# A down projection turned round: activations as the loaded weights, w_down moving, output by token

## Chip, cores and metric

The kernel runs on one core of a Trainium2 chip. The metric is the device time of one execution in microseconds. All times inside the program are counted from the start of the profiled span.

## What is computed

One transformer block over 2048 tokens of 1024 features, in float32: a modulated norm, a mixer of attention over compressed, selected and windowed keys beside a gated linear recurrence, and a feed-forward network with a causal convolution. Six modulation vectors come from one small product. The part that matters here is the end:

```python
mod = (c_act @ ada_w[l] + ada_b[l])[:, None, :]
sh1, sc1, g1, sh2, sc2, g2 = jnp.split(mod, 6, axis=-1)
...
x = x + g1 * (mixed @ w_out[l])
h = _rmsnorm(x, ffn_norm_g[l]) * (1.0 + sc2) + sh2
x = x + g2 * _conv_ffn(h, ffn_w_gate[l], ffn_w_up[l], ffn_conv_w[l], ffn_conv_b[l], ffn_w_down[l])
return _rmsnorm(x, final_norm_g)
```

`_conv_ffn` convolves `h @ w_gate` (2816 features, width 3), takes its silu, multiplies by `h @ w_up` and projects with `w_down` back to 1024 features.

## The kernel before

The program has three stages: the projections (pool "a"), attention with the output projection (pool "t"), and the feed-forward network (pool "f", from line 910). Tokens go in 4 chunks of 512 (`TC`), features in blocks of 128 (`P`).

Every float32 product is made of three matmuls (`mm3`, line 127): each operand is split into a high part (rounded to the matmul's format) and a low part, and high×high, high×low and low×high are summed in PSUM. `split` (line 120) makes the parts: ScalarE copies the high one, VectorE or GpSimd subtracts for the low one. `pe.matmul(ps, a, b)` loads `a` (128×128) as weights and moves `b` through; the trace and the order name the moving operand first (`pd<-gh,wd_0h`: gh moves, wd_0h is loaded).

A chunk of the feed-forward stage runs so:

- 22 blocks f of the gate and up products (lines 931 to 953). `wload` (918) fetches 512 KB of weights on SP's queue and splits it, the low part on GpSimd. Weights are the loaded operand, the normed input `hT` (8 pairs of 128×512) moves; results are features × tokens, in PSUM banks "g" and "u". The convolution, silu and product (940 to 952) leave pairs `gT` (gh, gl), features × tokens.
- the norm of the next chunk's input (`norm_T`, 161, and `norm_k`, 149): x is loaded by tokens, transposed by TensorE into bank "t", scaled into the next `hT`.
- the down projection (963 to 976): for each of 8 blocks d of output features, two weight loads of 704 KB, 66 matmuls with `gT` moving into one bank "d" (features × tokens). ScalarE copies the bank to `yT`, scaled by the column g2. TensorE transposes yT in four 128×128 pieces into bank "t", and VectorE adds each to `O`, the residual by tokens.
- the final norm (978 to 999): after block 6 and again after block 7, squares on ScalarE, a GpSimd power for 1/rms, the gains, and the store of `O`.

The modulation products run as small steps in the projection stage (`ada_steps`, 187, two per call of `ada_next`): steps b = 16 to 23 (g1) make a row, broadcast over 128 partitions by a matmul with ones, and store it to DRAM (`G1_d`); the others make columns of `mod`, among them b = 40 to 47 (g2).

The order of instructions on each engine is set by a scheduler that simulates the program (`schedule_with_timeline_sim`), not by the source. Each engine, and SP's queue of transfers, then runs its list in order; an instruction that waits holds up what is behind it. Tiles with one tag share `bufs` buffers; a new one waits until the oldest is released.

Of the kernel before, what the change touches and what calls it, by code (L numbers as in the profile page):

```python
# [38 lines left out]
ROW = {"gate_b": (0, 24), "cb2v": (24, 88), "fng": (88, 88 + D), "ada_g1": (88 + D, 88 + 2 * D)}  # L39
NROW = 88 + 2 * D  # L40
# [13 lines left out]
def hymba_block(ctx, tc, x, vecs, rows, ada, w_in, w_v, lru_w, cmp_w1, cmp_w2, w_out, w_gu, w_dn,  # L54
# [43 lines left out]
    G1_d = dr.tile([P, D], F32, name="G1_d")  # L98
    cact = cst.tile([P, KT], F32, name="cact")
# [49 lines left out]
    def norm_k(pl, pp, xs, c, k, Acol, Bcol, hbufs):  # L149
        ps = pp.tile([P, TC], F32, name=f"tp{c}_{k}", tag="t", bufs=2)  # L150
# [36 lines left out]
    def ada_steps(pl, pp, caz, b):  # L187
# [5 lines left out]
        if 16 <= b < 24:  # L193
            ps = pp.tile([P, P], F32, name=f"ap{b}", tag="g", bufs=2)
            pe.matmul(ps, ones, r, start=True, stop=True)
            gsl = slice((b - 16) * P, (b - 15) * P)
            ar = pl.tile([P, P], F32, name=f"ar{b}", tag="adrow", bufs=1)
            o = ROW["ada_g1"][0] + (b - 16) * P
# [711 lines left out]
    with tc.tile_pool(name="f", bufs=1, reuse_waits="tile") as pl, tc.tile_pool(name="fp", bufs=1, space=PSUM, reuse_waits="tile") as pp:  # L910
        reserve(pl, ("hh", 2048, 8), ("hl", 2048, 8), ("x", 4096, 6), ("hf", 2048, 2), ("junk", 2048, 1),
                ("raw", 512 * (NF // 2), 2), ("wh", 512 * (NF // 2), 2), ("wl", 512 * (NF // 2), 2),
                ("gp", 4 * (TC + 2), 2), ("ac", 2048, 2))
        B2, g2 = mod[:, 24:32], mod[:, 40:48]
# [14 lines left out]
        for c in range(NCH):  # L929
            gT = []  # L930
            for f in range(NF):
                lo_eng = dve if c == 0 and f == 0 else None
                wg = wload(w_gu[f, 0], KT, f"wg{c}_{f}", lo_eng)
                pg = pp.tile([P, TC], F32, name=f"pg{c}_{f}", tag="g", bufs=2)
                mm3(pg, [((wg[0][:, k], wg[1][:, k]), hT[k]) for k in range(KT)], 0, 24)
                wu = wload(w_gu[f, 1], KT, f"wu{c}_{f}", lo_eng)
# [17 lines left out]
            if c + 1 < NCH:  # L954
                hT = norm_T(pl, pp, X_d, c + 1, A2, B2, 6, 8)
            if c == 0:
                fng = pl.tile([P, D], F32, name="fng")
                row(fng, "fng")
            O = [pl.tile([P, D], F32, name=f"o{c}_{t}", tag="x", bufs=6) for t in range(4)]
            for t in range(4):  # L960
                sync.dma_start(O[t], X_d[c * TC + t * P:c * TC + (t + 1) * P, :])
            sss = []
            for d in range(KT):
                pd = pp.tile([P, TC], F32, name=f"pd{c}_{d}", tag="d", bufs=2)
                n = 0
# [12 lines left out]
                if d < KT - 2:  # L978
                    continue
                cs = slice(0, D - P) if d == KT - 2 else slice(D - P, D)  # L980
                n = d - (KT - 2)
                for t in range(4):
                    if n == 0:
                        ss = pl.tile([P, 2], F32, name=f"fs{c}_{t}", tag="fs", bufs=4)
                        sss.append(ss)
                    ss = sss[t]
                    junk = pl.tile([P, D], mybir.dt.bfloat16, name=f"fj{c}_{t}_{n}", tag="junk", bufs=1)
                    act.activation(junk[:, cs], O[t][:, cs], AF.Square, accum_out=ss[:, n:n + 1])
                    if n == 0:
                        pool.tensor_tensor(O[t][:, cs], O[t][:, cs], fng[:, cs], op=OP.mult)  # L990
                    else:
                        pool.tensor_tensor(ss[:, 0:1], ss[:, 0:1], ss[:, 1:2], op=OP.add)  # L992
                        r = rstd_of(ss[:, 0:1], D, pl, f"fr{c}_{t}")
                        dve.scalar_tensor_tensor(O[t][:, cs], O[t][:, cs], r, fng[:, cs], op0=OP.mult, op1=OP.mult)
                        if t % 2:
                            act.activation(O[t][:, 0:D - P], O[t][:, 0:D - P], AF.Copy, scale=r)
# [82 lines left out]
```

## Time and profile before

| | us |
|---|---|
| median of 3 runs | 2939.94 |
| lowest and highest | 2930.49, 2944.06 |
| profiled execution | 2934.73 |
| its span | 2933.0 |
| TensorE busy in the span | 2832.0 (97%) |
| granted clock, mean | 0.993 |

The profile shows one execution. Engines are PE (TensorE; PEld its weight loads), DVE (VectorE), ACT (ScalarE), POOL (GpSimd), SP (queue of transfers). A matmul's row lasts longer than the distance to the next one's start, because matmuls overlap in the array; rates are read from starts. An arrow in brackets in a row names what ended an engine's idle time before it.

### The profile page before, as it was taken

What the parts mean: (1) busy time and instruction counts of PE and PEld (TensorE: products, weight loads), DVE (VectorE), ACT (ScalarE), POOL (GpSimd) and SP (SyncE); (2) the same over time, 40 slices, a digit from 0 to 9 for tenths busy, and PEclk for the clock granted to TensorE, in tenths of its full rate; (3) what the DMA queues carried; (4) which work ended last, traced back from release to release, by engine and by line L of the source; (5) the groups of instructions that cost most, each with busy time, mean ns of one, the idle gap of its engine ahead of it and who ended that gap; (6) DMA issues with size and microseconds to landing.
All of it is one profiled execution on the core that took longest, in us unless ns stands there. A gap on an engine that the chain in (4) does not pass through costs nothing. (4 is left out here: it accounts for less than half of the span.)

```text
span 2933.0 us, 40574 instructions
## 1 busy us (share of the span) xinstructions
PE 2832.0 (97%) x14436; PEld 2328.3 (79%) x14436; DVE 1694.0 (58%) x3149; ACT 1497.8 (51%) x2686; POOL 1322.3 (45%) x1392
## 2 busy tenths in 40 slices
PE   8999999889999899999999999999999999999998
PEld 6777778777778777888788888888887888888886
DVE  4656657776777888888566621666216662166610
ACT  5656566586777777777633333433334333233322
POOL 1111010166666556565344445544455444554444
PEclk9999999999999999999999999999999999999999
DMA  7576655764544434433533333433324333243332
GB/s 285 177 268 203 242 196 151 225 164 129 138 137 121 123 111 111 116 110 96 190 94 96 104 118 98 140 99 96 128 86 151 94 103 121 88 135 100 97 105 78
DMA packets 256617, 397.89 MB, mean 136 GB/s; under 512 B 41376, under 2 KB 168352, under 8 KB 256416
## 3 DMA queue, kind: packets, MB, share of 16 engines
q1 hardware_dynamic: 255808, 394.12, 43.5%
q8 instruction: 115, 1.88, 0.3%
q0 software_dynamic: 320, 1.05, 0.1%
q14 instruction: 86, 0.70, 0.1%
q10 hardware_dynamic: 288, 0.13, 0.0%
HBM read 342.15 MB, written 53.08 MB: 135 GB/s over the span
## 5 line engine op out<-in xcount | busy, mean ns | idle before, releaser
L787 DVE TENSOR_TENSOR tl<-pt,th 128x512 fp32r<-128x512 f32 (+4 forms) x444 | 295.2, 684 | 46.9 <-ACT th L786 45.0
L944 DVE TENSOR_SCALAR ac<-gp,vec 128x512 f32<-128x512 f32 x88 | 188.5, 2143 | 215.6 <-ACT gp L941 208.5
L786 ACT ACTIVATE th<-pt 128x512 fp32r<-128x512 f32 (+4 forms) x444 | 255.1, 594 | 103.2 <-PE pt L785 98.4
L976 DVE TENSOR_TENSOR o<-pt,o 128x128 f32<-128x128 f32 x128 | 28.3, 284 | 433.1 <-PE pt L973 433.1
L757 POOL TENSOR_SCALAR ps<-ps,rs,gates 128x1024 f32<-128x1024 f32 (+7 forms) x192 | 182.0, 958 | 160.3 <-DVE rs L754 116.4
L952 DVE TENSOR_TENSOR gl<-ac,gh 128x512 fp32r<-128x512 f32 x88 | 209.5, 2381 | 69.4 <-ACT gh L951 69.4
L947 ACT ACTIVATE ac<-ac 128x512 f32<-128x512 f32 x88 | 55.7, 633 | 310.7 <-DVE ac L946 310.7
L751 ACT ACTIVATE ps<-ps,mn 128x1024 f32<-128x1024 f32 (+7 forms) x192 | 171.5, 897 | 51.6 <-DVE mn L651 51.3
L785 PE MATMUL pt<-ident,ps 128*128 128x128 f32 x1088 | 167.4, 275 | 7.8 <-DVE tl L787 6.5
L785 PEld LDWEIGHTS pt<-ident,ps 128*128 128x128 f32 x1088 | 133.0, 141 | 44.1 <-DVE tl L787 13.0
L124 POOL TENSOR_TENSOR wd_0l<-wd,wd_0h 128x1408 fp32r<-128x1408 f32 x32 | 103.1, 3223 | 139.8 <-ACT wd_0h L123 139.8
L646 PE MATMUL ss<-ks,Q 128*128 128x512 f32 (+3 forms) x640 | 162.2, 374 | 4.0 <-DVE mn L651 2.1
L124 POOL TENSOR_TENSOR wd_1l<-wd,wd_1h 128x1408 fp32r<-128x1408 f32 x32 | 103.2, 3224 | 130.8 <-ACT wd_1h L123 113.7
L946 DVE SCALAR_TENSOR_TENSOR ac<-gp,vec,ac 128x512 f32<-128x512 f32 x176 | 136.3, 774 | 6.1
L131 PE MATMUL pd<-gl,wd_0h 128*128 128x512 f32 x352 | 139.7, 397 | 0.0
L646 PEld LDWEIGHTS ss<-ks,Q 128*128 128x128 f32 x640 | 114.5, 191 | 30.1 <-issue 4.4
L131 PE MATMUL pd<-gh,wd_0h 128*128 128x512 f32 x352 | 137.9, 392 | 0.0
L131 PE MATMUL pd<-gl,wd_1h 128*128 128x512 f32 x352 | 137.7, 391 | 0.0
L131 PE MATMUL pd<-gh,wd_0l 128*128 128x512 f32 x352 | 137.5, 391 | 0.0
L131 PE MATMUL pd<-gh,wd_1l 128*128 128x512 f32 x352 | 137.3, 390 | 0.0
L131 PE MATMUL pd<-gh,wd_1h 128*128 128x512 f32 x352 | 137.2, 390 | 0.0
L123 ACT ACTIVATE wd_0h<-wd 128x1408 fp32r<-128x1408 f32 x32 | 44.2, 1383 | 158.2 <-PE pd L131 99.8
(1557 smaller groups left out, 8621.8 us busy)
## 6 DMA issues: line engine op xcount, KB each, us to landing
wg<-in_w_gu_dram SPq DMA_DIRECT2D x88, 512.0 KB, 3.6
wu<-in_w_gu_dram SPq DMA_DIRECT2D x88, 512.0 KB, 3.6
wd<-in_w_dn_dram SPq DMA_DIRECT2D x64, 704.0 KB, 4.1
wr<-in_w_in_dram SPq DMA_DIRECT2D x64, 512.0 KB, 5.1
ad<-in_ada_dram SPq DMA_DIRECT2D x32, 512.0 KB, 4.8
Q<-Q_d SPq DMA_DIRECT2D x64, 256.0 KB, 4.5
ks<-K_d SPq DMA_DIRECT2D x56, 256.0 KB, 3.4
vs<-V_d SPq DMA_DIRECT2D x56, 256.0 KB, 3.1
```

What stands on the lines that cost most here:

```text
L124: (lo_eng or dve).tensor_tensor(l, raw, h.bitcast(F32), op=OP.subtract)
L131: pe.matmul(ps, a, b, start=(n == 0), stop=(n == total - 1))
L646: pe.matmul(ps[:, o:o + W], Qt[:, hl, h * P:(h + 1) * P], K_ap, start=(hl == 0), stop=(hl == 1))
L751: act.activation(p, p, AF.Exp, scale=-1.0, bias=init, accum_out=sm[:, h, 2 + n:3 + n])
L757: pool.tensor_scalar(p, p, rs[:, h, 2:3], gt[:, h, 1:2], op0=OP.mult, op1=OP.mult)
L785: pe.transpose(pt[:, h * P:(h + 1) * P], jobs[n][0](h), ident)
L786: act.activation(th, pt, AF.Copy)
L787: dve.tensor_tensor(tl, pt, th.bitcast(F32), op=OP.subtract)
L944: dve.tensor_scalar(ac, gp[:, 0:TC], V("fcw", f), V("fcb", f), op0=OP.mult, op1=OP.add)
L946: dve.scalar_tensor_tensor(ac, gp[:, k:k + TC], V("fcw", k * NF + f), ac, op0=OP.mult, op1=OP.add)
L947: act.activation(ac, ac, AF.Silu)
L952: dve.tensor_tensor(l, ac, h.bitcast(F32), op=OP.subtract)
```

## The change

The down projection is turned round. `gT` slices (128 features × 128 tokens) are the loaded operand and `w_dn` moves, 512 output features at a time. The result is tokens × features, so the transposes go. The output features are done in two halves; in a half, four banks (one per block of 128 tokens) are summed over 11 weight tiles of 2 × 128 rows × 512 columns (512 KB). The first half uses four banks "d", the second the banks "g" and "u" of the gate and up products. The transposes of the next input go to bank "g". The gate g2 now multiplies as a row: modulation steps 40 to 47 make it as 16 to 23 did, and it is read to `g2b` once. Weight tiles have three buffers instead of two.

```diff
+    G2_d = dr.tile([P, D], F32, name="G2_d")
...
-        if 16 <= b < 24:
+        if 16 <= b < 24 or b >= 40:
             ps = pp.tile([P, P], F32, name=f"ap{b}", tag="g", bufs=2)
             pe.matmul(ps, ones, r, start=True, stop=True)
...
-            sync.dma_start(G1_d[:, gsl], ar)
+            sync.dma_start((G1_d if b < 24 else G2_d)[:, gsl], ar)
...
+        reserve(pp, ("g", 2048, 2), ("u", 2048, 2), ("d", 2048, 4))
...
-                ("raw", 512 * (NF // 2), 2), ("wh", 512 * (NF // 2), 2), ("wl", 512 * (NF // 2), 2),
-                ("gp", 4 * (TC + 2), 2), ("ac", 2048, 2))
+                ("raw", 4096, 3), ("wh", 4096, 3), ("wl", 4096, 3), ("gp", 4 * (TC + 2), 2), ("ac", 2048, 2))
...
-                hT = norm_T(pl, pp, X_d, c + 1, A2, B2, 6, 8)
+                hT = norm_T(pl, pp, X_d, c + 1, A2, B2, 6, 8, "g")
...
-            for d in range(KT):
-                pd = pp.tile([P, TC], F32, name=f"pd{c}_{d}", tag="d", bufs=2)
-                n = 0
-                for hf in range(2):
-                    wd = wload(w_dn[d, hf], NF // 2, f"wd{c}_{d}_{hf}")
-                    n = mm3(pd, [((wd[0][:, k], wd[1][:, k]), gT[hf * (NF // 2) + k]) for k in range(NF // 2)], n, 3 * NF)
-                yT = pl.tile([P, TC], F32, name=f"yT{c}_{d}", tag="hf", bufs=2)
-                act.activation(yT, pd, AF.Copy, scale=g2[:, d:d + 1])
-                pt = pp.tile([P, TC], F32, name=f"pt{c}_{d}", tag="t", bufs=2)
+            sss = [pl.tile([P, 2], F32, name=f"fs{c}_{t}", tag="fs", bufs=4) for t in range(4)]
+            for hf in range(2):
+                cs = slice(hf * 512, (hf + 1) * 512)
+                pd = [pp.tile([P, 512], F32, name=f"pd{c}_{hf}_{t}", **(dict(tag="gu"[t // 2], bufs=2) if hf else dict(tag="d", bufs=4)))
+                      for t in range(4)]
+                for q in range(NF // 2):
+                    wd = wload(w_dn[hf, q], 2, 512, f"wd{c}_{hf}_{q}")
+                    for t in range(4):
+                        sl = slice(t * P, (t + 1) * P)
+                        mm3(pd[t], [((gT[2 * q + k][0][:, sl], gT[2 * q + k][1][:, sl]), (wd[0][:, k], wd[1][:, k]))
+                                    for k in range(2)], 6 * q, 3 * NF)
                 for t in range(4):
-                    pe.transpose(pt[:, t * P:(t + 1) * P], yT[:, t * P:(t + 1) * P], ident)
-                for t in range(4):
-                    sl = O[t][:, d * P:(d + 1) * P]
-                    dve.tensor_tensor(sl, pt[:, t * P:(t + 1) * P], sl, op=OP.add)
...
+                    y = pl.tile([P, 512], F32, name=f"y{c}_{hf}_{t}", tag="hf", bufs=2)
+                    dve.tensor_tensor(y, pd[t], g2b[:, cs], op=OP.mult)
+                    dve.tensor_tensor(O[t][:, cs], O[t][:, cs], y, op=OP.add)
...
-                    act.activation(junk[:, cs], O[t][:, cs], AF.Square, accum_out=ss[:, n:n + 1])
-                    if n == 0:
+                    act.activation(junk[:, cs], O[t][:, cs], AF.Square, accum_out=ss[:, hf:hf + 1])
+                    if hf == 0:
                         pool.tensor_tensor(O[t][:, cs], O[t][:, cs], fng[:, cs], op=OP.mult)
...
-    w_dn = tiles(f["ffn_w_down"], P).reshape(KT, P, 2, NF // 2, P).transpose(0, 2, 1, 3, 4)
+    w_dn = f["ffn_w_down"].reshape(NF // 2, 2, P, 2, 512).transpose(3, 0, 2, 1, 4)
```

What the change makes of the engines' lists, at three places.

First, TensorE in the down projection of the first chunk. Before, inside output block 1, the four transposes of block 0 (`pt<-ident,yT`):

```order
L131 MATMUL pd_1_18222<-gl_9_17083,wd_1_0h 128x512
L131 MATMUL pd_1_18222<-gh_9_17082,wd_1_0l 128x512
L973 MATMUL pt_0_18213<-ident,yT_0_18211 128x128 x4
L131 MATMUL pd_1_18222<-gh_10_17158,wd_1_0h 128x512
L131 MATMUL pd_1_18222<-gl_10_17159,wd_1_0h 128x512
L131 MATMUL pd_1_18222<-gh_10_17158,wd_1_0l 128x512
```

After, the same engine where the first half ends (bank of token block 3, weight tile 10) and the second begins (token block 0, weight tile 0):

```order
L132 MATMUL pd_0_3_18169<-wd_0_10l,gh_21_18022 128x512
L132 MATMUL pd_0_3_18169<-wd_0_10h,gl_21_18023 128x512
L132 MATMUL pd_1_0_18524<-wd_1_0h,gh_0_16426 128x512
L132 MATMUL pd_1_0_18524<-wd_1_0l,gh_0_16426 128x512
L132 MATMUL pd_1_0_18524<-wd_1_0h,gl_0_16427 128x512
L132 MATMUL pd_1_0_18524<-wd_1_0h,gh_1_16502 128x512
```

The operands have changed places, the transposes are gone, and half follows half with nothing between.

Second, TensorE behind the last up product (`pu_21`) of the first chunk, where the next input is transposed (`tp`, blocks 0 to 7). Before, blocks 0 and 1 had been transposed in the gate stage, and block 2 comes after two matmuls:

```order
L131 MATMUL pu_21_17959<-h0hl_16323,wu_21h 128x512
L131 MATMUL pu_21_17959<-h0hh_16322,wu_21l 128x512
L131 MATMUL pd_0_18132<-gh_0_16398,wd_0_0h 128x512
L131 MATMUL pd_0_18132<-gl_0_16399,wd_0_0h 128x512
L152 MATMUL tp_2_18056<-ident,x_0_17998 128x128
L152 MATMUL tp_2_18056<-ident,x_1_18007 128x128
L152 MATMUL tp_2_18056<-ident,x_2_18016 128x128
L152 MATMUL tp_2_18056<-ident,x_3_18025 128x128
```

After, blocks 0 and 1 stand right behind `pu_21`; block 2 comes 26 matmuls after them:

```order
L132 MATMUL pu_21_17987<-h0hh_16350,wu_21l 128x512
L153 MATMUL tp_0_18062<-ident,x_0_18026 128x128
L153 MATMUL tp_0_18062<-ident,x_1_18035 128x128
L153 MATMUL tp_0_18062<-ident,x_2_18044 128x128
L153 MATMUL tp_0_18062<-ident,x_3_18053 128x128
L153 MATMUL tp_1_18073<-ident,x_0_18026 128x128
L153 MATMUL tp_1_18073<-ident,x_1_18035 128x128
L153 MATMUL tp_1_18073<-ident,x_2_18044 128x128
L153 MATMUL tp_1_18073<-ident,x_3_18053 128x128
L132 MATMUL pd_0_0_18166<-wd_0_0h,gh_0_16426 128x512
```

Two groups of four have moved from the gate products to the start of the down projection.

Third, SP's queue in the third chunk of the projections (`ad` modulation weights, `wr` weights of the projections, `Q_d` and `L_d` stores). Before:

```order
L190 DMA ad_3352<-in_ada_dram 128x1024
L270 DMA wr_3829<-in_w_in_dram 128x1024
L435 DMA Q_d<-qs_3_3679 128x1x512 x2
L190 DMA ad_3407<-in_ada_dram 128x1024
L416 DMA L_d<-ls_0_3684 256x1x512
L270 DMA wr_4031<-in_w_in_dram 128x1024
L416 DMA L_d<-ls_1_3688 256x1x512
```

After:

```order
L191 DMA ad_3356<-in_ada_dram 128x1024
L202 DMA G_d<-ar_3313 128x128
L200 DMA ar_3371<-in_rows_dram 128x128
L271 DMA wr_3839<-in_w_in_dram 128x1024
L436 DMA Q_d<-qs_3_3689 128x1x512 x2
L191 DMA ad_3414<-in_ada_dram 128x1024
L417 DMA L_d<-ls_0_3694 256x1x512
L271 DMA wr_4047<-in_w_in_dram 128x1024
L202 DMA G_d<-ar_3371 128x128
L417 DMA L_d<-ls_1_3698 256x1x512
L417 DMA L_d<-ls_2_3702 256x1x512
L200 DMA ar_3429<-in_rows_dram 128x128
```

A store of the gate row and the load of the next bias row now stand between the weight loads, eight times in all.

## Rows read from the trace of the kernel before

**Rows 1.** The page, parts 1 and 2: busy us (share) xinstructions; clock in tenths.

```profile
PE 2832.0 (97%) x14436; PEld 2328.3 (79%) x14436; DVE 1694.0 (58%) x3149; ACT 1497.8 (51%) x2686; POOL 1322.3 (45%) x1392
...
PEclk9999999999999999999999999999999999999999
```

**Rows 2.** Busy time by stretch, feed-forward stage: columns as in the first row.

```profile
core 0: us, PE busy (x) PEld busy (x) DVE busy (x) ACT busy (x) POOL busy (x), PEclk, DMA share, GB/s
...
1446.00:2933.00 1487.00, 1467.59 (x6562) 1210.20 (x6560) 658.37 (x619) 516.63 (x691) 734.00 (x505) 1.00 0.34 108
```

**Rows 3.** Waits of PE, 1440 to 2933: us in total, times, longest.

```profile
PE tp L152 <- DVE hf L157: 1.6, 3, 0.5
...
PE pu L131 <- POOL wu_2l L124: 1.3, 1, 1.3
PE pu L131 <- POOL wu_1l L124: 1.1, 2, 0.6
PE pg L131 <- POOL wg_3l L124: 1.1, 2, 0.5
```

**Rows 4.** Timeline of PE in the down projection: start, us, engine, instruction.

```profile
1715.97 0.40 PE L131 MATMUL pd<-gh,wd_1h 128*128 128x512 f32 x1
...
1720.06 0.39 PE L131 MATMUL pd<-gh,wd_1h 128*128 128x512 f32 x1
```

**Rows 5.** Timeline of PE at the last output projection (weights wo moving).

```profile
1432.95 2.90 PE L131 MATMUL p<-wo,lt 128*128 128x512 f32 x12
```

**Rows 6.** All instructions of tile pt: ns min/median/max, first and last start; waits.

```profile
L973 PE MATMUL pt<-ident,yT x128: 270/272/327, 1714.8 to 2921.6; 128*128 128x128 f32 x128
L976 DVE TENSOR_TENSOR o<-pt,o x128: 280/282/294, 1715.5 to 2922.5; 128x128 f32<-128x128 f32 x128
...
  PE pt L973: 433.1, 32
```

**Rows 7.** Timeline of PE round one group of output transposes.

```profile
1714.60 0.40 PE L131 MATMUL pd<-gh,wd_0l 128*128 128x512 f32 x1
...
1714.84 0.60 PE L973 MATMUL pt<-ident,yT 128*128 128x128 f32 x4
...
1715.19 0.48 PE L131 MATMUL pd<-gh,wd_0h 128*128 128x512 f32 x1
...
1715.51 0.40 PE L131 MATMUL pd<-gl,wd_0h 128*128 128x512 f32 x1
1715.74 0.39 PE L131 MATMUL pd<-gh,wd_0l 128*128 128x512 f32 x1
```

**Rows 8.** Timeline of the tail; last, line L988 by itself (squares of 896 and 128).

```profile
2920.01 0.39 PE L131 MATMUL pd<-gh,wd_1l 128*128 128x512 f32 x1
...
2922.73 0.19 POOL L992 TENSOR_TENSOR fs<-fs 128x1 f32<-128x1 f32 x1 [1.15 <-ACT fj L988]
...
2923.43 0.55 POOL L117 TENSOR_TENSOR fr<-fr,nhalf 128x1 f32<-128x1 f32 x1
...
2928.05 1.04 ACT L996 ACTIVATE o<-o,fr 128x896 f32<-128x896 f32 x1 [1.32 <-POOL fr L117]
...
L988 ACT ACTIVATE fj<-o x32: 310/624/954, 1808.0 to 2923.6; 128x896 bf16<-128x896 f32 x16, 128x128 bf16<-128x128 f32 x16
```

**Rows 9.** Lines of the gate stage on VectorE and GpSimd: ns min/median/max.

```profile
L952 DVE TENSOR_TENSOR gl<-ac,gh x86: 678/2477/3295, 1484.9 to 2800.8; 128x512 fp32r<-128x512 f32 x86
...
L948 DVE TENSOR_TENSOR ac<-ac,pu x86: 676/689/691, 1483.4 to 2799.0; 128x512 f32<-128x512 f32 x86
...
L124 POOL TENSOR_TENSOR wg_4l<-wg,wg_4h x4: 2393/2393/2395, 1489.4 to 2597.1; 128x1024 fp32r<-128x1024 f32 x4
```

**Rows 10.** Modulation steps, projection stage: row matmul, column matmul, store, wait for row load.

```profile
L195 PE MATMUL ap<-adrb,ones x16: 270/275/377, 78.7 to 157.8; 128*128 128x128 f32 x16
...
L182 PE MATMUL apc<-ones,adrb x48: 164/260/373, 162.1 to 470.5; 128*128 128x1 f32 x48
...
L201 SPq DMA_DIRECT2D G_d<-ar x8: 326/340/1694, 79.8 to 158.4; - x8
...
  DMA ar<-in_rows_dram: 5.6, 1
```

More of the change, by code (lines that the diff above doesn't have):

```diff
@@ L38 @@
 NVEC = _o
[L39 to L40 removed]
+ROW = {"gate_b": (0, 24), "cb2v": (24, 88), "fng": (88, 88 + D), "ada_g1": (88 + D, 88 + 2 * D), "ada_g2": (88 + 2 * D, 88 + 3 * D)}
+NROW = 88 + 3 * D
 CW = 164
@@ L147, in norm_x, with norm_k @@
         return xs
-    def norm_k(pl, pp, xs, c, k, Acol, Bcol, hbufs):
-        ps = pp.tile([P, TC], F32, name=f"tp{c}_{k}", tag="t", bufs=2)
+    def norm_k(pl, pp, xs, c, k, Acol, Bcol, hbufs, bank="t"):
+        ps = pp.tile([P, TC], F32, name=f"tp{c}_{k}", tag=bank, bufs=2)
         for t in range(4):
@@ L159, in norm_k, with norm_T @@
         return h, l
-    def norm_T(pl, pp, src, c, Acol, Bcol, xbufs, hbufs, xs=None, jt=("junk", 1)):
-        xs = xs or norm_x(pl, src, c, xbufs, jt)
-        return [norm_k(pl, pp, xs, c, k, Acol, Bcol, hbufs) for k in range(KT)]
+    def norm_T(pl, pp, src, c, Acol, Bcol, xbufs, hbufs, bank):
+        xs = norm_x(pl, src, c, xbufs)
+        return [norm_k(pl, pp, xs, c, k, Acol, Bcol, hbufs, bank) for k in range(KT)]
     def ada_product(pl, pp, caz, raws, name):
@@ L958, in hymba_block @@
                 row(fng, "fng")
+                g2b = pl.tile([P, D], F32, name="g2b")
+                sync.dma_start(g2b, G2_d)
             O = [pl.tile([P, D], F32, name=f"o{c}_{t}", tag="x", bufs=6) for t in range(4)]
@@ new lines, in hymba_block @@
+            sss = [pl.tile([P, 2], F32, name=f"fs{c}_{t}", tag="fs", bufs=4) for t in range(4)]
[9 more added lines that the diff above has]
+                                    for k in range(2)], 6 * q, 3 * NF)
+                for t in range(4):
+                    y = pl.tile([P, 512], F32, name=f"y{c}_{hf}_{t}", tag="hf", bufs=2)
+                    dve.tensor_tensor(y, pd[t], g2b[:, cs], op=OP.mult)
+                    dve.tensor_tensor(O[t][:, cs], O[t][:, cs], y, op=OP.add)
+                    junk = pl.tile([P, D], mybir.dt.bfloat16, name=f"fj{c}_{t}_{hf}", tag="junk", bufs=1)
@@ L986, in hymba_block @@
                     ss = sss[t]
-                    junk = pl.tile([P, D], mybir.dt.bfloat16, name=f"fj{c}_{t}_{n}", tag="junk", bufs=1)
-                    act.activation(junk[:, cs], O[t][:, cs], AF.Square, accum_out=ss[:, n:n + 1])
-                    if n == 0:
+                    act.activation(junk[:, cs], O[t][:, cs], AF.Square, accum_out=ss[:, hf:hf + 1])
+                    if hf == 0:
                         pool.tensor_tensor(O[t][:, cs], O[t][:, cs], fng[:, cs], op=OP.mult)
[L991 to L996, printed above, removed]
-                        else:
-                            dve.tensor_scalar(O[t][:, 0:D - P], O[t][:, 0:D - P], r, None, op0=OP.mult)
-                        sync.dma_start(out[c * TC + t * P:c * TC + (t + 1) * P, :], O[t])
+                        continue
@@ L1002, in _masks @@
+                    pool.tensor_tensor(ss[:, 0:1], ss[:, 0:1], ss[:, 1:2], op=OP.add)
+                    r = rstd_of(ss[:, 0:1], D, pl, f"fr{c}_{t}")
+                    dve.scalar_tensor_tensor(O[t][:, cs], O[t][:, cs], r, fng[:, cs], op0=OP.mult, op1=OP.mult)
+                    act.activation(O[t][:, 0:512], O[t][:, 0:512], AF.Copy, scale=r)
+                    sync.dma_start(out[c * TC + t * P:c * TC + (t + 1) * P, :], O[t])
 def _masks():
@@ L1038, in _layout @@
     vecs = np.concatenate([vec[n] for n, _ in VEC_WIDTHS], 1)
-    rows = np.concatenate([f["nsa_gate_b"], f["cmp_b2"][1], f["final_norm_g"], f["ada_b"][2 * D:3 * D]])[None, :]
+    rows = np.concatenate([f["nsa_gate_b"], f["cmp_b2"][1], f["final_norm_g"], f["ada_b"][2 * D:3 * D],
+                           f["ada_b"][5 * D:6 * D]])[None, :]
     def tiles(w, n):
```

24 lines of the change are left out of this document (8 added, 16 removed).

## Prediction

> **What bounds the kernel now.** I read the engine table first: TensorE is busy 97% of the span, VectorE 58%, the others less [rows 1]. Since busy time of overlapping matmuls says little, I then split the span: from 1446 us to the end, the feed-forward stage that the change edits, TensorE is busy 1467.6 of 1487 us at full granted clock (1.00, the 2.4 GHz level), while VectorE, ScalarE and GpSimd have more than half of it free [rows 2]. The stage is a queue of matmuls. So the price of an edit is what it does to the spacing of matmul starts, and what other engines do costs nothing until it holds a matmul up.
>
> The waits of TensorE in that stage are few: the transposes of the next chunk's input wait 1.6 us in all for VectorE, three times, and the first matmuls of a chunk wait 1.3 + 1.1 + 1.1 us for the low halves of weights that GpSimd makes [rows 3]. That is 5.1 us out of 1487.
>
> **The matmuls that stay.** Per chunk the down projection has 8 × 22 × 3 = 528 matmuls before and 2 × 4 × 11 × 2 × 3 = 528 after, all of a 128×128 weight load and 512 moving columns. Before, 19 of them in a row start between 1715.97 and 1720.06 [rows 4]: 4.09 / 18 = 0.227 us each. The new orientation (activations loaded, weights moving) is also in the trace: the output projection runs 12 such matmuls in 2.90 us [rows 5]; less the 0.39 us that one matmul's row lasts, (2.90 − 0.39) / 11 = 0.228. I take no difference. The two roundings leave about 0.001 us, over 4 × 528 = 2112 matmuls 2 us either way.
>
> **What is removed: the output transposes.** 128 of them ran, four after each of 32 output blocks [rows 6]. Their row lasts 0.272 us, but they overlap. I price a group from starts: the matmul before it starts at 1714.60 and the third one after that at 1715.74 [rows 7]. That is 1.14 us, where three steps of 0.227 would take 0.68: a group costs 0.46 us. All but the last group stand between matmuls: 31 × 0.46 = **14.2 us** off. The 32nd belongs to the tail, below. The gated copy on ScalarE and the 128 adds on VectorE go too; VectorE waited 433.1 us for those transposes [rows 6], so it was idle there and nothing is gained.
>
> The Trainium skill ("TensorE: Matmul & The Clock Gate", part 4 on transposes) gives about 275 ns for a transpose in a kernel. By that the 128 would be worth 35 us and the kernel would end near 2896 us. The duration of the row agrees with it, the spacing does not, so I keep 14.2 and make the full duration a rival.
>
> **Weight loading.** Three weight buffers of 512 KB replace two that held up to 704 KB. A gate or up weight can be loaded and split one tile earlier, and the transposes of the next input now begin right behind the last up product, with 26 matmuls (5.9 us) until the third of them asks for a bank again; before, it asked two matmuls behind that product (second excerpt of the order above). So the 5.1 us of waits [rows 3] should mostly go. I take **4 us**; bounds 0 and 5.1.
>
> **The tail.** The last matmul starts at 2920.01, the last arithmetic ends at 2928.05 + 1.04 = 2929.09 [rows 8]: 9.1 us. After the change the last token block needs the matmul's 0.39, a multiply out of PSUM (0.69, as the like one of the gate stage [rows 9]), an add (0.68, the shortest two-input row there), a square of 512 (half way between 0.31 for 128 and 0.95 for 896 [rows 8]: 0.63), three small GpSimd steps (2922.73 to 2923.43 + 0.55: 1.25 [rows 8]), and a scaling, again 0.69: 4.3 us. The other three blocks finished 1.4 to 4.1 us earlier and still have operations in the queue; I add three of 0.69. That gives 6.4, so **2.7 us** less. Bounds: 0, and 4.8 if nothing queues ahead.
>
> **What is added.** Eight modulation steps (b = 40 to 47, in the projection stage, third and fourth chunk) now make a gate row as b = 16 to 23 did. Their matmul is nearly as long (0.275 for 0.260 us, two per step [rows 10]), but each brings a row load and a store on SP's queue. The store waits for the add on VectorE, and the next row load waits for that store, since there is one buffer. Behind them stand weight loads, modulation loads and the compression loads (third excerpt). In the first chunk the same eight cost one wait of 5.6 us on VectorE, and one of the eight store issues took 1.69 instead of 0.34 us [rows 10]. I take **+3 us** for the eight. Bounds: 0, since weight loads run ahead, and 8 × 5.6 = 45.
>
> The fetch of the gate row to SBUF (512 KB, once) waits for nothing late; SP has all of the first gate stage for it. On VectorE the change puts 32 multiplies and 32 adds. The multiply reads PSUM and one SBUF tile. The add reads two SBUF tiles, and such an operation waits for GpSimd: the low-half subtraction on two SBUF tiles in the gate stage has a median of 2.48 us and a maximum of 3.30, where its shortest is 0.68, and GpSimd's own split takes 2.39; the multiply with a PSUM operand stays between 0.68 and 0.69 [rows 9]. The old adds read PSUM and took 0.28 [rows 6].
>
> The Trainium skill ("SBUF — State Buffer", section on the two sides) says that VectorE and GpSimd hold a shared port as a lock for a whole instruction and the loser waits it out. The trace agrees, by the 2.48 against 0.69; it speaks against this change.
>
> What the added waiting does to TensorE, for the turn from the first to the second half: the first block's sum is done 18 matmuls (4.1 us, less 0.39) before the turn. Four multiplies and four adds at the median take 4 × (0.69 + 2.48) = 12.7, so the last add ends 9.0 us after the turn. Then the square (0.63), a weight copy that stood behind it on ScalarE (at most GpSimd's 2.39), the gain multiply and the split on GpSimd (2.39 each at most): 16.8 as the worst sum. The weight tile concerned is the fourth of the half, due after 3 × 24 × 0.227 = 16.3. So it just holds when the steps cost what they should, and I charge **0**. The d banks are not needed until the next chunk; of the other four, the first is due at once and is freed by the first multiply, 3 us ahead.
>
> **Sum.** −14.2 − 4 − 2.7 + 3 = −17.9 us. Against the profiled execution (span 2933.0, 2934.73 with what lies around it) that is 2916.8. The median of the three runs, 2939.94, lies 5.2 above that execution, which would give 2922. I put down **2919**, between them.
>
> **Rivals.** (a) *The add behind GpSimd holds up the splits.* At the maximum of 3.30 the same sum is 3.3 us longer, 20.1 against 16.3 due: about 3.8 us at each of 7 turns (the last half has none behind it), 27 us, and 2943; a typical mixture of waits gives half of that, 2930. It begins to count once an add costs over 2.4 us. For it: the median above. Against: GpSimd works only 2.39 of every 5.4 us here, and nothing else runs on VectorE. (b) *A transpose is worth its duration:* 128 × 0.272 = 34.8 instead of 14.2, so 2896 to 2898. Against it stand the starts in [rows 7]. (c) *The row steps block SP,* the slower side: each of the eight makes the loads behind it late by 5.6 us, 45 in all instead of 3, and the kernel comes to 2919 + 42 = 2961. It is slower than before from 20.9 / 8 = 2.6 us a step on. For it: VectorE's wait in [rows 10]. Against: eight steps cost only one such wait in the first chunk. That the transposes would not go is excluded by the order: TensorE's list has none.
>
> **Chances.** Forecast 0.64 (2907 to 2926), rival (a) 0.22, (b) 0.05, (c) 0.09. A run of this kernel differs from its median by up to 0.3%, so about 0.5%, 14.7 us, can be told from no change: below 2925 is faster, above 2955 slower. Faster: 0.58 of the 0.64, plus 0.05, plus a little of (a): 0.65. Slower: most of (c), 0.07. The rest, 0.28, is the same. The range takes in the forecast's own bounds (all waits gone, the shorter tail: 2906) and the common part of (a): 2905 to 2938.
>
> **What would show it.** No transposes of the output and the 0.227 spacing in the down stage; no wait for a weight split at the chunk turns; matmul starts unbroken from half to half; from the last matmul to the last arithmetic about 6.4 us. Wrong: waits of down matmuls for GpSimd's splits at the turns (a); spacing unchanged but over 25 us gained in that stage (b); a later end of the projection stage than now, with TensorE waiting for modulation or weight loads (c).

## The result, and the profile after

| | before | after |
|---|---|---|
| median of 5 runs, side by side | 2939.94 us | 2916.53 us |
| lowest and highest | 2930.49, 2944.06 | 2909.66, 2920.84 |
| profiled execution, span | 2934.73, 2933.0 | 2917.85, 2916.1 |

The ratio is 0.9927, 95% interval 0.9914 to 0.994: faster by 0.6 to 0.9%. The forecast was 2919 us, with a range of 2905 to 2938.

The page's part 1 and the busy times by stretch, kernel after (the columns of the second line are those of [rows 2]):

```profile
PE 2821.5 (97%) x14308; PEld 2324.5 (80%) x14308; DVE 1723.8 (59%) x3077; ACT 1484.6 (51%) x2686; POOL 1319.2 (45%) x1416
...
1455.00:2916.00 1461.00, 1448.40 (x6435) 1198.85 (x6433) 686.91 (x547) 503.70 (x690) 731.84 (x529) 1.00 0.36 110
```

TensorE has 128 matmuls fewer, the output transposes. The feed-forward stage takes 1461 us instead of 1487 [rows 2], 26 less, but it begins at 1455 instead of 1446. So the profile holds a gain of 26 and a loss of 9, against a forecast of 21 and 3.

TensorE's waits from 1440 on, kernel after (in total, times, longest):

```profile
PE pg L132 <- DVE wg_0l L125: 1.5, 1, 1.5
PE pu L132 <- POOL wu_1l L125: 0.8, 1, 0.8
PE p L132 <- ACT pt L831: 0.6, 1, 0.6
```

The first two stand in the stage's first 21 us, the third in the output projection ahead of it. The waits of [rows 3] for the transposes' buffers and at the chunk turns are gone. The turn between two halves, timeline of TensorE, kernel after:

```profile
2123.61 0.39 PE L132 MATMUL pd<-wd_10l,gh 128*128 128x512 f32 x1
2123.84 0.39 PE L132 MATMUL pd<-wd_10h,gl 128*128 128x512 f32 x1
2124.06 0.39 PE L132 MATMUL pd<-wd_0h,gh 128*128 128x512 f32 x1
2124.29 0.39 PE L132 MATMUL pd<-wd_0l,gh 128*128 128x512 f32 x1
```

The starts keep their 0.227 across it, as in [rows 4]. VectorE's lines, kernel after (ns min/median/max, then first and last start):

```profile
L978 DVE TENSOR_TENSOR y<-pd,g2b x32: 676/682/692, 1757.6 to 2906.8; 128x512 f32<-128x512 f32 x32
...
L979 DVE TENSOR_TENSOR o<-o,y x32: 678/693/2052, 1758.3 to 2908.0; 128x512 f32<-128x512 f32 x32
```

The multiply costs what was taken for it. The add has a median of 0.69 us, not the 2.48 of [rows 9]; its mean is 1.07, because the first add at each of the seven turns lasts about 2 us and two more at a half turn 1.07. The tail, timeline, kernel after:

```profile
2905.38 0.39 PE L132 MATMUL pd<-wd_10h,gl 128*128 128x512 f32 x1
...
2911.31 0.75 DVE L988 SCALAR_TENSOR_TENSOR o<-o,fr,fng 128x512 f32<-128x512 f32 x1 [0.72 <-POOL fr L118]
```

From the last matmul's start to the last arithmetic's end are 2911.31 + 0.75 − 2905.38 = 6.7 us (forecast 6.4; before 9.1 [rows 8]).

**Where the stage's 26 us are.** From the first gate matmul to the last down matmul I summed what exceeds 0.2267 us between neighbouring starts, and put it down by what stands between (the first step behind a group of transposes, 0.32 us, counts to the group):

| us | before | after | difference |
|---|---|---|---|
| groups of output transposes (31 between matmuls) | 13.94 | 0 | −13.9 |
| spacing of the other matmuls | 1.77 | 0.07 | −1.7 |
| stalls (gaps over 0.24) | 7.96 | 3.18 | −4.8 |
| transposes of the next input | 14.02 | 10.65 | −3.4 |
| from the last down matmul to the end | 13.01 | 10.77 | −2.2 |

Of the 1.7 us of spacing, 1.0 lay behind the output transposes, whose next ten matmuls started up to 0.009 us further apart than 0.227 each; the rest lay behind the next input's transposes and behind waits.

**The early loss.** The row steps stand in the third and fourth chunk of the projections. Kernel before, then kernel after, timeline of TensorE: the first matmul of the third chunk, and the first of the attention stage.

```profile
290.06 0.48 PE L131 MATMUL zc<-hh,w36h 128*128 128x512 f32 x1
...
568.75 1.61 PE L646 MATMUL sa<-K,Q 128*128 128x340 f32 x8 [3.97 <-DMA K<-K_d]
```

```profile
289.38 0.48 PE L132 MATMUL zc<-hh,w36h 128*128 128x512 f32 x1
...
576.19 1.19 PE L647 MATMUL sa<-K,Q 128*128 128x340 f32 x3 [4.61 <-DMA K<-K_d]
```

That stretch went from 278.7 to 286.8 us. Line L201 in it, kernel after:

```profile
  DMA ar<-in_rows_dram: 16.9, 4
who waited for it (us, times):
  PEld pg L132: 2.7, 1
  PE pg L132: 2.4, 1
```

VectorE waits 16.9 us for the row loads, where the first chunk's eight steps cost 5.6 [rows 10], and a gate matmul of this stage (`pg`) waits 2.4 us behind that.

### The profile page after: what moved, and what is told of

Read it like the earlier page. It is cut to its first block, busy times and chain, and to the rows that moved or that the text cites. A ratio compares the mean times of both kernels' runs of the same rounds, so it can differ in the third digit from the quotient of the medians.

```text
span 2916.1 us, 40471 instructions
## 1 busy us (share of the span) xinstructions
PE 2821.5 (97%) x14308; PEld 2324.5 (80%) x14308; DVE 1723.8 (59%) x3077; ACT 1484.6 (51%) x2686; POOL 1319.2 (45%) x1416
## 4 chain that ended last, share of the span: by engine, by line
PE 80%; DVE 6%; ACT 5%; DMA 5%; issue 2%; POOL 1%; SPq 1%; POOLq 0%; DVEq 0%; ACTq 0%
PE pg L132 17%; PE pd L132 16%; PE pu L132 16%; PE p L132 6%; PE pt L786 5%; PE ss L647 3%; PE po L797 3%; PE po L798 3%; PE zy L132 2%; PE zx L132 2%; PE sa L647 2%; DMA xf<-C_d 1%; DVE tl L788 1%; PE zq L132 1%; ACT th L787 1%
## 5 line engine op out<-in xcount | busy, mean ns | idle before, releaser
L978 DVE TENSOR_TENSOR y<-pd,g2b 128x512 f32<-128x512 f32 x32 | 21.9, 683 | 371.1 <-PE pd L132 371.1
L798 PE MATMUL po<-tl,vs 128*128 128x512 f32 x272 | 123.6, 454 | 1.0 <-DVE tl L788 1.0
L797 PE MATMUL po<-th,vs 128*128 128x512 f32 x272 | 111.3, 409 | 6.4 <-ACT th L787 6.3
L652 DVE CUSTOM_DVE_ANT_1 ps<-ss,bi 128x1024 f32<-128x1024 f32 (+4 forms) x96 | 105.6, 1106 | 15.6 <-PE ss L647 10.3
L647 PE MATMUL sa<-K,Q 128*128 128x272 f32 (+14 forms) x464 | 99.1, 341 | 14.8 <-DVE mn L652 5.6
L786 PE MATMUL pt<-ident,pc 128*128 128x128 f32 (+9 forms) x688 | 103.7, 277 | 5.6 <-POOL pc L724 2.8
L726 POOL TENSOR_SCALAR pc<-pc,rs,gates 128x640 f32<-128x640 f32 (+4 forms) x128 | 104.2, 815 | 8.1 <-DVE mn L652 7.5
L401 POOL COPY hcar<-xc 128x1 f32<-128x1 f32 x16 | 19.4, 1212 | 180.7 <-DVE xc L400 180.0
L786 PEld LDWEIGHTS pt<-ident,pc 128*128 128x128 f32 (+9 forms) x688 | 81.7, 137 | 23.6 <-POOL pc L724 3.3
L949 DVE TENSOR_TENSOR ac<-ac,pu 128x512 f32<-128x512 f32 x88 | 60.5, 688 | 67.3 <-ACT ac L948 65.9
```

The costliest lines, as they stand in the source:

```text
L647: pe.matmul(ps[:, o:o + W], Qt[:, hl, h * P:(h + 1) * P], K_ap, start=(hl == 0), stop=(hl == 1))
L786: pe.transpose(pt[:, h * P:(h + 1) * P], jobs[n][0](h), ident)
L797: pe.matmul(po, jobs[n][1], th, start=(n == 0), stop=False)
L798: pe.matmul(po, jobs[n][1], tl, start=False, stop=(n == N - 1))
```

## Experiments

Theory: the stage gains by spacing (transposes), by waits of TensorE and by the tail, and loses to the row steps. Rivals: a transpose is worth its duration; the adds hold up the splits; the early loss is spread between executions.

**The same kernels again.** No edit.

> The changed kernel once more, for its spread. In the first pair of profiles the first feed-forward matmul started 9.2 us later after the change (1455.33 against 1446.18) while the feed-forward stage got 26.0 us shorter. Theory (the row steps cost it): again 1455, within 2 us, and again a time of 0.9927 of before, about 2917. Rival (the projection and attention stages differ from execution to execution): the start falls anywhere from 1446 to 1456, and the length of the feed-forward stage alone, 1460.8, repeats within 2 us.

> The kernel before, unchanged, for a second profile. Its first profiled execution (2934.73) was below its median (2939.94) and had the first feed-forward matmul at 1446.18; the kernel with columns and without a row of the second gate (cols) had it at 1452.97, and all with the row steps between 1455.3 and 1461.4. Theory (the first profile of before fell on a short early part): the start comes near 1451 and the feed-forward stage again takes 1486.8, within 1 us. Rival (the start is a fixed 1446 for this program and the whole 9.2 us are the change's): 1446, within 1 us.

> The changed kernel beside the two others on the same chip, for a difference of 5 us out of 2916. Expected: again 0.992 of before, 2916 to 2917, first attention matmul between 573 and 576, feed-forward stage 1460.8.

Measured: after 2916.27 (ratio 0.992, 0.9902 to 0.9937) and 2913.51 (0.992, 0.9905 to 0.9935). The stage took 1460.8 us in all three profiles of after, 1486.8 and 1485.9 in the two of before. The stage's start was 1455.7 and 1457.7 after, 1449.5 in the second profile of before. So the 26 is firm. Of the 9, some 3 were the first profile's short early part, as the theory for before had it.

The stretch from the third chunk to the first attention matmul separates better than the start does: in all profiles with column steps alone (both of before, and cols, cols2 and cols3 below) it took 278.7, 278.1, 280.5, 276.5 and 280.0, mean 278.8; in the six with the changed kernel's row steps and their loads 286.8, 283.3, 285.6, 284.8, 283.6 and 283.2, mean 284.6; VectorE's wait for the row loads was 16.9 to 17.6 us in these six. **The row steps cost 5.8 us there**, not 9 and not 3. The attention stage between that and the feed-forward stage took 877 to 883 us in both sets, but for cols2 (890.4, explained below).

**The row steps alone.**

```diff
-        if 16 <= b < 24:
+        if b >= 40:
+            ada_columns(pp, r, b, 1, 1, f"c{b}")
+        if 16 <= b < 24 or b >= 40:
...
-            sync.dma_start(G1_d[:, gsl], ar)
+            sync.dma_start((G1_d if b < 24 else G2_d)[:, gsl], ar)
```

> The kernel before with the eight row steps added to its eight column steps: the second gate row is made and stored, and nothing reads it; the rest is unchanged. It prices the row steps alone. Theory (they cost what the first pair of profiles shows): the first feed-forward matmul at 1455 instead of 1446, total 2949, ratio 1.003. The prediction's price: +3, 2943, ratio 1.001. Its rival (c): 45 us, 2985, ratio 1.015. In all cases the feed-forward stage itself keeps its 1486.8 us. Eight more small products for both forms add at most 16 x 0.275 = 4.4 us, mostly beside other waits.

Measured: 2948.23, ratio 1.0029 (1.0015 to 1.0042), 8.7 us over before. Timeline of TensorE, then one of its waits between 290 and 580 us, kernel before with row steps:

```profile
289.22 0.48 PE L132 MATMUL zc<-hh,w36h 128*128 128x512 f32 x1
...
576.32 0.86 PE L649 MATMUL sa<-K,Q 128*128 128x340 f32 x4 [3.79 <-DMA K<-K_d]
```

```profile
PE pg L132 <- DVE ar L203: 3.7, 2, 3.3
```

The stretch is 287.1, 8.3 over the columns' mean. This kernel makes the small products in both forms, the other two in one; that is at most 4.4 of it, so 3.9 to 8.3 are the steps' own. The feed-forward stage begins at 1461.4, later than the 1455 expected, since the attention stage took 885.1 here. Rival (c), 45, falls.

**Without the row loads.**

```diff
-            sync.dma_start(ar, bass.AP(tensor=rows.tensor, offset=rows.offset + o, ap=[[0, P], [1, P]]))
-            dve.tensor_tensor(ar, ps, ar, op=OP.add)
+            if b < 24:
+                sync.dma_start(ar, bass.AP(tensor=rows.tensor, offset=rows.offset + o, ap=[[0, P], [1, P]]))
+                dve.tensor_tensor(ar, ps, ar, op=OP.add)
+            else:
+                dve.tensor_copy(ar, ps)
```

> The changed kernel without the load of the bias row in the eight row steps of the second gate: VectorE copies the product instead of adding the row to it. It leaves the bias of the second gate out, so the output is another. The store of the row stays. Theory (the row loads, for which VectorE waited 16.9 us between 290 and 580 us, are what the row steps cost): the first attention matmul starts near 568 instead of 574, total 2911, ratio 0.990. Rival (the stores on SP, or the longer small products, cost it): it stays at 574, total 2917, ratio 0.992.

Measured: 2917.66, ratio 0.9931 (0.9915 to 0.9946). Timeline of TensorE, kernel without the row loads:

```profile
293.69 0.48 PE L132 MATMUL zc<-hh,w36h 128*128 128x512 f32 x1
...
571.87 4.45 PE L650 MATMUL sa<-K,Q 128*128 128x340 f32 x16 [3.74 <-DMA K<-K_d]
```

Two answers. The stretch is 278.2, the columns' length, though store and longer product stayed: by this one profile the loads are the whole cost there. But the first attention matmul starts at 571.9, between the theory's 568 and the rival's 574, and the total is the rival's 2917, 4.2 over the changed kernel in the same comparison. The third chunk begins 4 us later than in the changed kernel, in code that the edit leaves alone, and the attention stage takes 884.6. Whether that is spread or comes with the edit is open, so the loads are the likely cause and not a shown one.

**Columns, and the row made later on TensorE.** Three versions of one idea; the first:

```diff
-        if 16 <= b < 24 or b >= 40:
+        if 16 <= b < 24:
...
-                sync.dma_start(g2b, G2_d)
...
+                for hf in range(2):
+                    dg = pl.tile([P, 4, P], F32, name=f"dg{hf}", tag="hf", bufs=2)
+                    for j in range(4):
+                        dve.tensor_scalar(dg[:, j], ident, mod[:, 40 + 4 * hf + j:41 + 4 * hf + j], None, op0=OP.mult)
+                    dh, dl = split(pl, dg, [P, 4, P], f"dg{hf}", "w", 3)
+                    pb = pp.tile([P, 4, P], F32, name=f"pb{hf}", tag="d", bufs=4)
+                    pe.matmul(pb, oner, dh, start=True, stop=False)
+                    pe.matmul(pb, oner, dl, start=False, stop=True)
+                    act.activation(g2b[:, hf * 512:(hf + 1) * 512], pb.rearrange("p a b -> p (a b)"), AF.Copy)
```

> The changed kernel, but the second gate is made as columns like before, without the eight row steps on SP; its row is built once at the start of the first down projection, from ones times a diagonal of the gate (4 matmuls of 512 columns, 4 x 0.227 = 0.9 us, if their operands are ready). Theory (row steps cost 9.2 us): first feed-forward matmul at 1446, total 2916.5 - 9.2 + 0.9 = 2908, ratio 0.989. By the prediction's price of 3: 2914, ratio 0.991. Rival (execution to execution spread): 2917, ratio 0.993, like the changed kernel. If the diagonal is late, TensorE shows a wait at the start of that down projection and up to 5 us of the gain go.

Measured: 2924.83, ratio 0.9946 (0.9931 to 0.9961), some 9 us *slower* than the changed kernel. The feed-forward stage began at 1453.0, not at the 1446 expected. Two of TensorE's waits in the stage, then its timeline at the start of the first down projection, kernel cols:

```profile
PE tp L153 <- DVE hf L158: 3.3, 6, 1.2
PE pb L969 <- ACT dg0h L124: 3.1, 1, 3.1
```

```profile
1707.41 0.79 PE L969 MATMUL pb<-dg0h,oner 128*128 128x512 f32 x1 [3.10 <-ACT dg0h L124]
```

Four matmuls worth 0.9 us made the stage 13.9 us longer. The diagonal took buffers of the next input's norm, and all 32 transposes of that input now stood in a row ahead of it: they waited 3.3 us, the clock fell to half among them (below), and the 3.1 us for the diagonal came on top. These waits and the matmuls make 7.3 of the 13.9; the other 6.6, an estimate by difference, are mainly rows at half the clock. The second version built the row from other buffers among the gate products, in program order:

```diff
+                if c == 0 and f in (10, 12):
...
+                    dx = pl.tile([P, 2, 4, P], F32R, name=f"dx{hf}", tag="x", bufs=6)
...
+                if c == 0 and f in (11, 13):
+                    pb = pp.tile([P, 4, P], F32, name=f"pb{hf}", tag="d", bufs=4)
```

> As cols, but the row of the second gate is built during the gate products of the first chunk (blocks 10 to 13), with its operands in buffers that are idle there, so that its 4 matmuls find them ready. Theory (in cols the late diagonal cost the feed-forward stage 1474.7 - 1460.8 = 13.9 us, of which only 0.9 is matmul time): that stage takes 1462, the early part stays as in cols, total 2924.8 - 12.7 = 2912, ratio 0.9906, some 4 us better than the changed kernel. Rival (the eight row steps cost nothing that a median shows): 2917, ratio 0.992, like the changed kernel.

Measured: 2915.56, ratio 0.9918 (0.9903 to 0.9933): the rival's figure, but not for the rival's reason. Timeline of TensorE, kernel cols2:

```profile
1449.59 0.50 PE L969 MATMUL pb<-dx,oner 128*128 128x512 f32 x1 [2.29 <-ACT dx L965]
...
1455.10 0.80 PE L132 MATMUL pg<-h0hh,wg_0h 128*128 128x512 f32 x1 [3.18 <-ACT wg_0h L124]
```

Nothing tied the row to block 10, so the scheduler put it ahead of the stage's first matmul. That waited 3.2 us for a weight copy, which stood behind the copies of the row's result (`g2b`) on ScalarE; 8.2 us lie between it and the last matmul ahead of the four. The third version takes buffers of the loop itself, which hold it in place (shown against the second):

```diff
-                    dg = pl.tile([P, 4, P], F32, name=f"dg{hf}", tag="hf", bufs=2)
+                    dg = pl.tile([P, 4, P], F32, name=f"dg{hf}", tag="ac", bufs=2)
...
-                    pb = pp.tile([P, 4, P], F32, name=f"pb{hf}", tag="d", bufs=4)
+                    pb = pp.tile([P, 4, P], F32, name=f"pb{hf}", tag="u", bufs=2)
```

> As cols2, but the scheduler is kept from moving the row's matmuls to the start of the stage: the diagonal now takes the buffers of the convolution's accumulator and the result a bank of the up product, so that the 4 matmuls stand between gate and up products of blocks 11 to 14. Theory: no row steps, so the first attention matmul starts near 568 (mean of the four runs with columns; 574 for the five with row steps, 5.9 later); 0.9 us of matmuls and no wait in the feed-forward stage (1461.7); total 2916.4 - 5.9 + 0.9 = 2911.4, ratio 0.990. Rival (what the row steps cost in the projection stage is made up in the attention stage): 2917, ratio 0.992, like the changed kernel.

Measured: **2909.84** (2907.25 to 2912.5), ratio 0.9906 (0.9892 to 0.9919). The one wait of TensorE in the stage, then half of the row's matmuls (ns min/median/max, first and last start), kernel cols3:

```profile
PE pg L132 <- DVE wg_0l L125: 1.5, 1, 1.5
```

```profile
L969 PE MATMUL pb<-dx,oner x2: 389/389/389, 1583.2 to 1605.4; 128*128 128x512 f32 x2
```

That is nearer the theory's 2911.4 than the rival's 2917, though the first attention matmul started at 571.9 and not near 568. This version is clearly faster than the kernel before. It lies 3.7 us under the changed kernel in the same comparison and 5.6 under the median of that one's 14 runs in three comparisons (2915.4); but the runs of the two overlap, and so do the intervals, so that it beats the changed kernel is likely and not shown.

**Transposes put back.** 32 groups whose result nobody reads.

```diff
+                    if hf == 0 and 1 <= q <= 8:
+                        dm = pp.tile([P, 512], F32, name=f"dm{c}_{q}", tag="u", bufs=2)
+                        for t in range(4):
+                            pe.transpose(dm[:, t * P:(t + 1) * P], ident, ident)
```

> The changed kernel with 32 groups of four 128x128 identity transposes put back between matmuls of the down projection, eight groups in each chunk's first half; their results are not read and they wait for nothing late, so they cost TensorE's time alone. Theory (a group is worth what the spacing of starts says, 0.45 to 0.46 us): +14.6 us over the changed kernel, 2931, ratio 0.997 of before. Rival (b) (a transpose is worth its row's 0.272 us): +34.8 us, 2951, ratio 1.004.

Measured: 2933.77, ratio 0.9974 (0.9963 to 0.9985), 17.5 us over the changed kernel; the stage is 15.6 us longer. Timeline of TensorE at one group, kernel with dummy transposes:

```profile
2090.86 0.39 PE L132 MATMUL pd<-wd_3h,gl 128*128 128x512 f32 x1
2091.09 0.60 PE L979 MATMUL dm<-ident 128*128 128x128 f32 x4
2091.44 0.48 PE L132 MATMUL pd<-wd_4h,gh 128*128 128x512 f32 x1
2091.76 0.40 PE L132 MATMUL pd<-wd_4l,gh 128*128 128x512 f32 x1
2091.99 0.40 PE L132 MATMUL pd<-wd_4h,gl 128*128 128x512 f32 x1
```

From 2090.86 to 2091.99 are 1.13 us where three steps take 0.68: 0.45 a group, as in [rows 7]. Over the stage it is 15.6 / 32 = 0.49, because the ten matmuls behind a group also start some thousandths of a us further apart (1.5 us over the stage). A transpose in such a group is worth 0.12 us, with a row of 0.272. Rival (b), 34.8, falls.

**Two weight buffers.**

```diff
-                ("raw", 4096, 3), ("wh", 4096, 3), ("wl", 4096, 3), ("gp", 4 * (TC + 2), 2), ("ac", 2048, 2))
+                ("raw", 4096, 2), ("wh", 4096, 2), ("wl", 4096, 2), ("gp", 4 * (TC + 2), 2), ("ac", 2048, 2))
...
```

> The changed kernel with two weight buffers of 512 KB instead of three; no arithmetic changes. It prices the third buffer alone. Theory (the third buffer is what took the waits for split weights away): they come back, the feed-forward stage gets 4 to 8 us longer, total 2920 to 2924, ratio 0.994. Rival (the smaller tiles or the place of the transposes did it): 0 to 1 us, 2917, ratio 0.992. A third possibility: with two buffers of 512 KB a tile of the down projection is split only 24 matmuls ahead (5.4 us), and waits appear in the down stage too: over 20 us, 2937 or more.

Measured: 2923.98, ratio 0.9949 (0.993 to 0.9968), 8.6 us over the 2915.4 of the changed kernel; the stage is 6.6 us longer. TensorE's larger waits in it, kernel with two buffers:

```profile
PE pg L132 <- POOL wg_1l L125: 2.9, 4, 1.2
PE pg L132 <- DVE wg_0l L125: 1.5, 1, 1.5
PE pg L132 <- ACT wg_1h L124: 1.3, 1, 1.3
PE pu L132 <- ACT wu_1h L124: 0.7, 1, 0.7
```

The stage's start and the chunk turns wait for splits again; the down stage has no wait. By the sum over starts, 5.6 us of stalls are back and 0.5 of spacing, but only 0.1 at the next input's transposes. So the third buffer took the stalls away. The 3.4 us at the next input's transposes stay gone without it: 2.1 us of waits for their buffers, and 1.1 that the matmuls behind them lose less. That they come from the transposes' new place among the matmuls is read from the order; the bank changed with it, and neither was tried alone.

**Longer evictions.**

```diff
                     dve.tensor_tensor(y, pd[t], g2b[:, cs], op=OP.mult)
+                    for _ in range(3):
+                        dve.tensor_tensor(y, y, y, op=OP.max)
```

> The changed kernel with three more operations on VectorE (maximum of y with itself, 0.68 us each) before each of the 32 residual adds; the result is the same. The last add of a half comes 8.2 us later. Theory (the chain behind the adds has a few us of slack: 5.4 at a half turn and 2.4 at a chunk turn, by the trace of the changed kernel): 4 x (8.2 - 5.4) + 3 x (8.2 - 2.4) = 28.6 us of waits at the turns and 2 to 8 at the end, together 31 to 37, 2950, ratio 1.004; TensorE waits for GpSimd's splits there. Rival (the adds are off the path, whatever they take): only the end, 2 to 8 us, 2919 to 2925, ratio 0.994.

Measured: 2927.14, ratio 0.9959 (0.9944 to 0.9973), 11.7 us over the changed kernel: in the profile 8.3 in the tail and 4.0 in the stage, behind the chunk turns. Both expectations fall, the theory's by far. TensorE's waits in the stage, kernel with longer evictions:

```profile
PE pg L132 <- POOL wg_3l L125: 2.7, 2, 1.5
PE pg L132 <- DVE wg_0l L125: 1.5, 1, 1.5
PE pu L132 <- POOL wu_1l L125: 0.8, 1, 0.8
```

Nothing waits at a half turn, although the last add there ends 16.1 us after the turn instead of 3.6: the extra operations took up to 2.88 us where GpSimd worked too. GpSimd's split of the fourth weight tile, timeline, first the changed kernel, then this one:

```profile
2132.41 2.39 POOL L125 TENSOR_TENSOR wd_3l<-wd,wd_3h 128x1024 fp32r<-128x1024 f32 x1
```

```profile
2132.98 2.83 POOL L125 TENSOR_TENSOR wd_3l<-wd,wd_3h 128x1024 fp32r<-128x1024 f32 x1
```

It ends 5.8 us before its matmul in the changed kernel (2140.6) and still 4.2 before it here (2140.0). The instruction list of ScalarE tells more: first the changed kernel, then this one, at the first half turn.

```
L124 ACTIVATE wd_1_1h<-wd_1_1_18558 128x1024
L982 ACTIVATE fj_0_0_18503,fs_0_18162<-o_0_18154 128x512
L982 ACTIVATE fj_1_0_18509,fs_1_18163<-o_1_18155 128x512
L124 ACTIVATE wd_1_2h<-wd_1_2_18588 128x1024

L124 ACTIVATE wd_1_1h<-wd_1_1_18570 128x1024
L124 ACTIVATE wd_1_2h<-wd_1_2_18600 128x1024
L984 ACTIVATE fj_0_0_18506,fs_0_18162<-o_0_18154 128x512
L984 ACTIVATE fj_1_0_18515,fs_1_18163<-o_1_18155 128x512
```

With later adds the third weight copy moved ahead of the squares, and in the trace the fourth runs ahead of the last two squares, where it stood behind all four. The fifth still stands behind all four:

```profile
2141.88 2.40 POOL L125 TENSOR_TENSOR wd_4l<-wd,wd_4h 128x1024 fp32r<-128x1024 f32 x1
```

Its split ends 1.2 us before its matmul (2145.4), against 7.3 in the changed kernel. So later adds do press on the splits, and the margin is nearly used up here. The slack was computed for a fixed order, but the order is made anew for each kernel.

## Why the prediction came out

Term by term, from the table, the stretches and the tail:

| term | forecast | measured |
|---|---|---|
| output transposes | −14.2 | −14.9 (13.9 at the groups, 1.0 behind them) |
| weight waits | −4, bounds 0 to −5.1 | −8.9 (4.8 stalls, 3.4 at the next input's transposes, 0.7 of spacing behind both) |
| tail | −2.7 | −2.2 |
| row steps | +3 | +5.8 |
| sum | −17.9 | −20.2 |

- **Transposes, right.** Pricing from starts held to a tenth: 14.9 us here, and 15.6 for the 32 groups put back. The figure of the Trainium skill ("TensorE: Matmul & The Clock Gate", part 4) of about 275 ns for a transpose in a kernel is the row's length here too (0.272). It is not what 128 of them cost between matmuls, 15.6 us and not 35.
- **Weight waits, mechanism right, size off.** The step "That is 5.1 us out of 1487" summed some rows of the list of waits. The list holds 8.3 in the stage; the rows left out, kernel before:

```profile
PE pg L131 <- DVE wg_0l L124: 1.5, 1, 1.5
...
PE pu L131 <- ACT wu_1h L123: 0.9, 1, 0.9
PE pt L973 <- ACT yT L970: 0.8, 1, 0.8
```

The first stayed, the second went, and the third, which lay in the tail, went with the transposes. And a wait costs more than its row: those for weights are 5.9 us in the list, but the starts showed 8.0 of stalls, with the step behind a wait at 0.34 us instead of 0.227. The starts also showed 14.0 at the next input's transposes, which the step priced by their waits of 1.6 alone. From 5.1 the bound of the gain was set, and 8.9 went.

- **Row steps, size off.** The step "the same eight cost one wait of 5.6 us on VectorE" was carried over from the first chunk as one wait of the eight, cut to 3. In the later chunks four waits came, 16.9 us on VectorE, and 5.8 reached the end of the stage. The two misses went opposite ways, so the total is closer than its terms.
- **Tail, right:** 6.7 us against 6.4.
- **The half turn, right in its zero, wrong in its sum.** The sum came to 16.8 against a due time of 16.3, so by its own figures it did not quite hold, and it was charged 0 all the same. The step "Four multiplies and four adds at the median" took 2.48 us for an add. At the half turn of the second chunk the four last 1.98, 0.69, 1.07 and 1.07: the last add ends 3.6 us after the turn, not 9.0, and the split has 5.8 us to spare. Rival (a) has no cost here. The Trainium skill ("SBUF — State Buffer", the two sides) describes a lock between VectorE and GpSimd. The trace agrees in kind, with up to 2.05 us for adds whose shortest is 0.68, but a median belongs to the stage it was read in: the two-input subtraction of the gate stage stays at a mean of 2.38 in the same kernel.
- **The range.** Its lower end, 2906, does not follow from the terms: with all waits gone, the shorter tail and row steps at 0, the execution of 2934.73 gives 2910.6. The measured time lies above both.

The medians differ by 23.3 to 24.1 us in the three comparisons, the terms give 20.2. The 3 to 4 us between were not traced: the profiled executions of before lie 3 to 5 us under its medians, those of the changed kernel 1 to 7 over its own, and the attention stage alone varies by 5 between profiles. That the forecast came within 3 us of the median is therefore in part luck; the mechanisms and their signs are not.

## What to carry to other kernels

Price what stands in a stream of matmuls by the distance of starts round it, and sum the stalls the same way: the waits for weights were 5.9 us in the list and 8.0 in the starts. And sum the whole list, not some of its rows. Price a small serial step by the stretch it is moved into, not by the stretch where it ran before; here eight steps with a 64 KB load each, on a busy queue, cost 6 us. And when a row or a constant is built in spare time, tie it to buffers of the loop, or look up where the scheduler put it: the same four matmuls cost 14 us, 8 us, or nothing that shows.

## What was not expected of the hardware

TensorE's clock fell within a row of transposes that had short waits between them. Kernel cols, timeline of TensorE, then busy time and clock by stretch (columns as in [rows 2]):

```profile
1694.42 1.03 PE L153 MATMUL tp<-ident,x 128*128 128x128 f32 x8
...
1697.94 0.66 PE L153 MATMUL tp<-ident,x 128*128 128x128 f32 x4 [0.60 <-DVE hf L158]
...
1700.42 1.12 PE L153 MATMUL tp<-ident,x 128*128 128x128 f32 x4 [0.34 <-DVE hf L158]
```

```profile
1698.00:1699.00 1.00, 0.59 (x4) 0.35 (x4) 0.66 (x1) 1.00 (x3) 0.00 (x0) 1.00 0.00 0
1700.00:1702.00 2.00, 1.46 (x6) 0.98 (x6) 1.12 (x2) 1.94 (x4) 0.00 (x0) 0.50 0.00 0
...
1711.00:1716.00 5.00, 4.77 (x11) 3.39 (x12) 0.00 (x0) 1.11 (x2) 5.00 (x3) 0.50 0.47 130
1717.00:1720.00 3.00, 3.00 (x15) 2.48 (x14) 0.00 (x0) 0.25 (x1) 0.00 (x0) 1.00 0.73 194
```

From 1694.4 TensorE ran nothing but the 32 transposes, with waits of 1.2 to 0.2 us between groups of four. The granted clock was 1.00 until 1699 and 0.50, the 1.2 GHz level, from 1700, and a group then took 1.12 us instead of 0.66. That was 4 us before the wait for the diagonal began (1704.3), so that wait did not bring it down. The clock was still 0.50 while the matmuls ran again, with rows of 0.63 instead of 0.39, and 1.00 from 1717. The dummy transposes, which stood between matmuls without waits, left it at 1.00. In cols2, too, the clock had fallen before the wait of 3.2 us: the last of the row's matmuls ahead of it already lasted 0.79.
